# A fused mixer layer on one core: GpSimd's two-input steps of a head pair and the output weights' buffers in the Projection stage

## The chip, the cores and the metric

The kernel runs on one core of a Trainium2 chip. The metric is the device time of one execution in microseconds (us). Before the change three runs took 1478.3, 1480.67 and 1480.91 us; the median is 1480.67 us. The engines are TensorE (PE; its weight loads are shown apart as PEld), VectorE (DVE), ScalarE (ACT), GpSimd (POOL) and SyncE (SP), which issues the transfers.

## The reference

One layer over 2048 tokens with 1024 features, all in float32. The input is normalised and multiplied by `w_in` (1024 x 3712); the columns of that product feed three mixers; their outputs, each gated, go through `w_out`, and a gated addition of a second input follows.

```python
h = rms_norm(x, pre_norm_g[i])
z = h @ w_in[i]
out_a = spatial_gating(u_a, v_a, ...) * silu(g_a)
out_b = conv_module(val_b, glu_b, ...) * silu(g_b)        # 31 taps
out_c = rwkv7_mix(z[..., oc:og], ...) * silu(z[..., og:]) # 8 heads of 64
mix = concatenate([out_a, out_b, out_c], -1) @ w_out[i]
x = x + rms_norm(mix, post_norm_g[i])
gate = sigmoid(x @ ple_gate_w[i] + ple_gate_b[i])
x = x + (p[i] @ ple_w[i]) * gate
```

In `rwkv7_mix` the columns r, k, v are first mixed with the token before (`z + mu * (prev - z)`); then `kk = k * k_k` is divided by its norm per head, `k` is scaled by `1 + (a - 1) * k_a`, and the scan over time takes `-kk`, `kk * a`, `k`, `v` and `r`.

## The kernel before

The program has three stages. **Projection** computes `z` and all that is made of it for the mixers. A second stage runs the scan in chunks of 64 tokens, and the last one multiplies by `w_out` and applies the gate. The change is in Projection only.

Projection works on two halves of 1024 tokens. `z` is made transposed, 128 columns by 1024 tokens, in 29 column tiles in the order of the list `ORDER` (2, 8, 3, 6, 24, 9, 7, 12, 16, 13, 20, 17, 21, 4, 14, ...). Tiles 2 and 3 are made by L312 (`gemm_t`) in another layout; every other one by L300 (`gemm1`) in 48 matmuls of 128 x 512. Each operand is held as the sum of a high and a low part of a shorter type, so a tile takes three products, and every operand must first be split: ScalarE copies the high part and a two-input subtraction makes the low one. For the weights this is done in half 0 (`load_w`, L282 on ScalarE and L283 on GpSimd); both parts go to DRAM (`w_s`), and half 1 reads them back (`again`, L292), two buffers of the pool `w` for each tile. The pool `w` has 6 buffers of 512 KB, so three tiles' weights fit. `z` has two PSUM buffers: the gemm of a tile can start only when every reader of the tile two places earlier is done.

What reads a tile differs. `s_prep` (one for each of the four head pairs and each half) takes the tiles of r, k and v: `shift` (L329 on ScalarE, L330 and L333 on VectorE) is the token shift, and about twenty elementwise steps follow, five of them on GpSimd in the kernel before: the low part of the squares `rn` (`parts`, L232), `rn * ic` (L522), `ks * ic` (L524), `ks * em` (L527) and the low part of `rs` (L232 again). `sums` (L240) multiplies such parts by a matrix of ones on TensorE. `s_lora` shifts tile 24 into a buffer of the pool `mk` and splits it (L424 to L431). `s_conv` multiplies a tile by its gate (L444) and adds 31 taps on VectorE (L449 and 30 times L453) for each of two tiles. `s_sgu` normalises tiles 2 and 3 (L583 to L587).

`s_wout` splits the output weights: eight parts of 128 x 1024, each loaded (L378), copied by ScalarE (L380), subtracted on GpSimd (L381) and both parts written to DRAM (L383). It does so at the start of half 1 in three buffers of the pool `mk` each; this pool has 8 buffers.

In Projection a scheduler sets the order in which each engine gets its instructions. Every one of these generators yields a due time in units of one tile (half 1 begins at `NG`, 29), and lowers it for what must be done early by `at(...)`: the readers of a `z` tile are put at its time minus 5. An engine runs its queue strictly in the order so made, and a buffer is given to its next user in that order too. From the second stage on the order of PE and DVE is written out.

Of the kernel before, what the change touches and what calls it, by code (L numbers as in the profile page):

```python
# [12 lines left out]
F32R = mybir.dt.float32r  # L13
AF = mybir.ActivationFunctionType
ALU = mybir.AluOpType
# [19 lines left out]
def hybrid_kernel(ctx, tc, x, x_t, w_in, vecs, wup, pw_w, sgu_wt, sgu_lnb, sgu_b,  # L35
                  w_out, post_g, p_t, ple_w, gate_w, gate_b, out):
    nc = tc.nc
# [17 lines left out]
    def nm(s):  # L55
        uid[0] += 1
        return f"{s}{uid[0]}"

    def new(tag, shape=(128, 1024), dt=F32):
        return sb.tile(list(shape), dt, tag=tag, bufs=BUFS[tag], name=nm(tag))  # L60
# [81 lines left out]
    def col(i):  # L142
        return vc[:, i:i + 1]
# [84 lines left out]
    def parts(src, eng):  # L228

        hl = [new("mk", dt=F32R) for _ in range(2)]  # L230
        nc.scalar.copy(hl[0], src)
        eng.tensor_tensor(out=hl[1], in0=src, in1=hl[0], op=ALU.subtract)  # L232
        return hl
# [93 lines left out]
    def shift(j, half, z, tag="L"):  # L327
        o = new(tag)
        nc.scalar.activation(o, z, AF.Identity, scale=om[:, j:j + 1])  # L329
        nc.vector.scalar_tensor_tensor(out=o[:, 1:], in0=z[:, :HT - 1], scalar=col(V_MU + j), in1=o[:, 1:],  # L330
                                       op0=ALU.mult, op1=ALU.add)
        if half == 1:
            nc.vector.scalar_tensor_tensor(out=o[:, 0:1], in0=zl[:, j:j + 1], scalar=col(V_MU + j),  # L333
                                           in1=o[:, 0:1], op0=ALU.mult, op1=ALU.add)
        else:
            nc.scalar.copy(zl[:, j:j + 1], z[:, HT - 1:HT])
        return o
# [4 lines left out]
    def split(dst_hi, dst_lo, src):  # L342

        nc.scalar.copy(dst_hi, src)
        nc.vector.tensor_tensor(out=dst_lo, in0=src, in1=dst_hi, op=ALU.subtract)
# [4 lines left out]
    NG = len(ORDER)  # L350
# [22 lines left out]

    def s_wout():
        for k in range(8):
            yield NG + 1.2 + 0.4 * k
            wr = new("mk")
            nc.sync.dma_start(out=wr, in_=w_out[k * 128:(k + 1) * 128, :])  # L378
            ws = [new("mk", dt=F32R) for _ in range(2)]
            nc.scalar.copy(ws[0], wr)  # L380
            nc.gpsimd.tensor_tensor(out=ws[1], in0=wr, in1=ws[0], op=ALU.subtract)  # L381
            for j in range(2):
                nc.sync.dma_start(out=wo_s[k, :, j], in_=ws[j].bitcast(F32))  # L383

# [71 lines left out]
    def s_prep(half, p, st):  # L456
# [6 lines left out]
        ic = new("mk")  # L463
# [20 lines left out]
        em = new("L")  # L484
# [5 lines left out]
        rs_ = shift(p, half, Z[half, 12 + p])  # L490
        yield b0 + TG[16 + p] + 0.1
        at(b0 + TG[16 + p] - 5)
        ks_ = shift(4 + p, half, Z[half, 16 + p])
        yield b0 + TG[16 + p] + 0.0

        rn = new("mk")
        nc.scalar.activation(rn, ks_, AF.Square, scale=col(V_KK + p))
        hl = parts(rn, nc.gpsimd)
        for g in range(2):
            sp = mps()  # L500
            sums(sp, ones64, [hl], slice(g * 512, (g + 1) * 512))
# [11 lines left out]
        for g in range(2):  # L513
# [3 lines left out]
                                           in1=ep[:, c8, 0:64], op0=ALU.mult, op1=ALU.mult)  # L517
# [1 line left out]
            c0 = 16 * half + 8 * g  # L519
            nc.sync.dma_start(out=ar_s[c0:c0 + 8, :, p, :].rearrange("c p s -> p c s"), in_=ar)  # L520

        nc.gpsimd.tensor_tensor(out=rn, in0=rn, in1=ic, op=ALU.mult)  # L522
        nc.scalar.activation(ic, ic, AF.Identity, scale=col(V_KA + p), bias=om[:, 13 + p:14 + p])
        nc.gpsimd.tensor_tensor(out=ks_, in0=ks_, in1=ic, op=ALU.mult)  # L524
        yield b0 + TG[20 + p] + 1.3
        nc.vector.tensor_tensor(out=rn, in0=rn, in1=em, op=ALU.mult)
        nc.gpsimd.tensor_tensor(out=em, in0=ks_, in1=em, op=ALU.mult)  # L527
        for par in range(2):
            lo = 64 * par
            dst = bk_s[16 * half:16 * half + 16, lo:lo + 64, p, :, :].rearrange("c p k s -> p k c s")  # L530
# [10 lines left out]
        for par in range(2):  # L541
            nc.sync.dma_start(
                out=v_s[t0:t0 + HT, par, p, :].rearrange("(i t) d -> t i d", t=128),
# [2 lines left out]

        nc.vector.scalar_tensor_tensor(out=rs_, in0=rs_, scalar=col(V_RK + p), in1=ks_,
                                       op0=ALU.mult, op1=ALU.mult)
        hl = parts(rs_, nc.gpsimd)
        for g in range(2):  # L550
            sp = mps()
            sl = slice(g * 512, (g + 1) * 512)
# [115 lines left out]

    S = []
    S += [s_weights(), s_wout(), s_x(), s_gemm(), s_silu(0), s_const()]  # L670
    for half in range(2):
        st = {}
        S += [s_lora(half, st), s_conv(half, 0, st), s_conv(half, 1, st)]
        S += [s_prep(half, p, st) for p in range(4)]
        S += [s_sgu(half, st), s_pw(half, st)]
# [677 lines left out]
```

## Time and profile before

| what | us |
|---|---|
| median of three runs | 1480.67 |
| the profiled execution's own time | 1478.66 |
| its span (first to last instruction) | 1476.9 |
| TensorE busy | 1386.2 |
| VectorE busy | 1000.6 |
| ScalarE busy | 573.7 |
| GpSimd busy | 374.0 |

The mean granted clock of TensorE was 0.977 of full speed. All times in the rows are counted from the start of the span. Half 0 of Projection runs to about 430 us (its last gemms still run beside the first work of half 1), half 1 to about 740 us. A timeline groups neighbouring instructions of one line: a row gives the start, the sum of their durations (with the gaps between them), the engine, line and operation, and in brackets the idle time of the engine before it and who released it. `z<-h,w` means a result in a buffer named z from buffers h and w.

### The profile page before, as it was taken

What the parts mean: (1) busy time and instruction counts of PE and PEld (TensorE: products, weight loads), DVE (VectorE), ACT (ScalarE), POOL (GpSimd) and SP (SyncE); (2) the same over time, 40 slices, a digit from 0 to 9 for tenths busy, and PEclk for the clock granted to TensorE, in tenths of its full rate; (3) what the DMA queues carried; (4) which work ended last, traced back from release to release, by engine and by line L of the source; (5) the groups of instructions that cost most, each with busy time, mean ns of one, the idle gap of its engine ahead of it and who ended that gap; (6) DMA issues with size and microseconds to landing.
All of it is one profiled execution on the core that took longest, in us unless ns stands there. A gap on an engine that the chain in (4) does not pass through costs nothing.

```text
span 1476.9 us, 24431 instructions
## 1 busy us (share of the span) xinstructions
PE 1386.2 (94%) x9701; PEld 1105.7 (75%) x9701; DVE 1000.6 (68%) x1955; ACT 573.7 (39%) x900; POOL 374.0 (25%) x332
## 2 busy tenths in 40 slices
PE   7998989999998499999899989999999989999998
PEld 6876767787796377778667777777777777888887
DVE  6599993674437999535975687787788653555553
ACT  6333344555331352634333435444543443212121
POOL 5432454541403303403320112202211100111110
PEclk9999999999999699999999989999999999999999
DMA  8332366679538415635842653323332443323231
GB/s 325 144 142 86 128 197 202 185 255 312 187 124 306 150 64 161 170 109 171 256 144 80 231 192 98 116 82 116 95 101 73 139 141 123 134 102 130 101 132 43
DMA packets 158312, 223.30 MB, mean 151 GB/s; under 512 B 58236, under 2 KB 108149, under 8 KB 158198
## 3 DMA queue, kind: packets, MB, share of 16 engines
q1 hardware_dynamic: 158066, 221.68, 45.3%
q8 instruction: 76, 1.25, 0.4%
q14 instruction: 38, 0.31, 0.1%
q10 hardware_dynamic: 132, 0.06, 0.0%
HBM read 132.58 MB, written 89.13 MB: 150 GB/s over the span
## 4 chain that ended last, share of the span: by engine, by line
PE 66%; DVE 26%; ACT 3%; issue 2%; DMA 2%; POOL 1%; DVEq 0%; ACTq 0%; POOLq 0%
PE z L300 26%; PE z L1165 12%; DVE inv L453 10%; PE z L1052 8%; PE c L1142 3%; PE z L312 3%; DVE inv L874 3%; PE m L821 2%; DVE inv L879 2%; DVE mk L245 2%; PE m L240 1%; DVE inv L862 1%; PE m L1121 1%; PE c L944 1%; PE c L932 1%
## 5 line engine op out<-in xcount | busy, mean ns | idle before, releaser
L300 PE MATMUL z<-h,w 128*128 128x512 f32 x2592 | 638.2, 401 | 31.4 <-DVE mk L330 23.2
L300 PEld LDWEIGHTS z<-h,w 128*128 128x128 f32 x2592 | 487.9, 190 | 152.2 <-DVE mk L330 23.6
L1052 PE MATMUL z<-h,w 128*128 128x512 f32 x768 | 206.4, 412 | 0.7 <-DVE w L1039 0.7
L453 DVE SCALAR_TENSOR_TENSOR inv<-inv,vc,inv 128x1024 f32<-128x1024 f32 x120 | 195.2, 1635 | 2.6
L1052 PEld LDWEIGHTS z<-h,w 128*128 128x128 f32 x768 | 140.1, 192 | 31.7 <-DVE w L1039 1.1
L283 POOL TENSOR_TENSOR w<-w,w 128x1024 fp32r<-128x1024 f32 x26 | 70.4, 2709 | 126.8 <-PE z L300 93.8
L1165 PE MATMUL z<-L,w 128*128 128x512 f32 (+1 forms) x384 | 96.1, 393 | 0.0
L1165 PE MATMUL z<-h,w 128*128 128x512 f32 (+1 forms) x384 | 93.6, 392 | 0.8 <-DVE inv L1148 0.8
L1109 POOL TENSOR_TENSOR inv<-inv,pg 128x1024 f32<-128x1024 f32 x16 | 38.5, 2405 | 216.3 <-DMA inv<-mx_s 141.3
L1149 ACT ACTIVATE inv<-inv 128x512 f32<-128x512 f32 (+1 forms) x33 | 20.4, 619 | 182.5 <-DVE inv L1148 182.5
L874 DVE TENSOR_TENSOR inv<-inv,inv 128x48 f32<-128x48 f32 (+23 forms) x464 | 85.8, 219 | 2.3
L879 DVE TENSOR_TENSOR inv<-inv,inv 128x48 f32<-128x48 f32 (+23 forms) x464 | 84.2, 217 | 1.2
L1165 PEld LDWEIGHTS z<-h,w 128*128 128x128 f32 x384 | 71.5, 189 | 17.3 <-DVE inv L1148 1.2
L1148 DVE TENSOR_TENSOR inv<-z,L 128x512 f32<-128x512 f32 (+1 forms) x32 | 21.9, 683 | 89.1 <-PE z L1165 89.1
L1165 PEld LDWEIGHTS z<-L,w 128*128 128x128 f32 x384 | 70.3, 188 | 15.2
L979 POOL TENSOR_TENSOR ri<-ri,pc 128x256 f32<-128x256 f32 x31 | 19.5, 628 | 239.6 <-DVE L L977 229.4
L245 DVE RECIPROCAL mk<-mk 128x256 f32<-128x256 f32 x40 | 65.9, 1709 | 17.5 <-ACT mk L504 9.5
L826 DVE TENSOR_TENSOR mk<-m,mask 128x512 f32<-128x512 f32 x58 | 37.6, 685 | 35.4 <-PE m L821 31.2
L830 ACT COPY inv<-mk 32x128 f32<-32x128 f32 x128 | 37.8, 295 | 52.1 <-DVE mk L826 49.3
L330 DVE SCALAR_TENSOR_TENSOR L<-z,vc,L 128x1023 f32<-128x1023 f32 x24 | 30.6, 1277 | 38.8 <-ACT L L329 36.6
L312 PE MATMUL z<-w,h 128*128 128x256 f32 x384 | 53.4, 295 | 0.9 <-ACT h L262 0.9
L329 ACT ACTIVATE L<-z,om 128x1024 f32<-128x1024 f32 x24 | 26.8, 1115 | 69.3 <-PE z L300 69.3
(246 smaller groups left out, 2067.5 us busy)
## 6 DMA issues: line engine op xcount, KB each, us to landing
w_s<-w SPq DMA_DIRECT2D x58, 512.0 KB, 3.4
w<-w_s SPq DMA_DIRECT2D x58, 512.0 KB, 5.0
w<-in_w_in_dram SPq DMA_DIRECT2D x26, 512.0 KB, 3.6
L<-in_x_dram SPq DMA_DIRECT2D x16, 512.0 KB, 8.1
ar_s<-L SPq DMA_DIRECT2D x16, 512.0 KB, 5.8
wo_s<-mk SPq DMA_DIRECT2D x16, 512.0 KB, 4.8
L<-ar_s SPq DMA_DIRECT2D x32, 256.0 KB, 3.1
L<-bk_s SPq DMA_DIRECT2D x32, 256.0 KB, 4.1
```

What stands on the lines that cost most here:

```text
L245: nc.vector.reciprocal(t[:, g * 256:(g + 1) * 256], t[:, g * 256:(g + 1) * 256])
L283: nc.gpsimd.tensor_tensor(out=ws[1], in0=wr, in1=ws[0], op=ALU.subtract)
L300: nc.tensor.matmul(z[:, g * 512:(g + 1) * 512], lhsT=ws[a][:, k * 128:(k + 1) * 128], rhs=h[:, b, k, :], start=(n == 0), stop=(n == 23))
L312: nc.tensor.matmul(z[:, i * 256:(i + 1) * 256], lhsT=h[:, b, k, i * 128:(i + 1) * 128], rhs=ws[k // 4][a][:, (k % 4) * 256:(k % 4 + 1) * 2 ...
L453: nc.vector.scalar_tensor_tensor(out=ac, in0=y[:, i:i + HT], scalar=col(V_CW + 2 * i + ct), in1=ac, op0=ALU.mult, op1=ALU.add)
L830: nc.scalar.copy(g["g"][32 * q:32 * q + 32, 0, 4 * ci:4 * ci + 4, :], mk[32 * q:32 * q + 32, par, :, s0:s0 + 32])
L874: nc.vector.tensor_tensor(out=tmp[:, o:o + n, :m], in0=tl[:, lo:hi, m:m + 1].to_broadcast([128, n, m]), in1=ml[:, m, :m].unsqueeze(1).to_b ...
L879: nc.vector.tensor_tensor(out=tl[:, lo:hi, :m], in0=tl[:, lo:hi, :m], in1=tmp[:, o:o + n, :m], op=ALU.add)
L1052: nc.tensor.matmul(mx[:, nh * 512:(nh + 1) * 512], lhsT=oT[a][:, k, :], rhs=wo[k // 4][:, b, k % 4, nh * 512:(nh + 1) * 512], start=(k == ...
L1109: nc.gpsimd.tensor_tensor(out=x2, in0=x2, in1=pg[0], op=ALU.mult)
L1142: nc.tensor.matmul(pp, lhsT=pT[:, a, k, :], rhs=gw[8 + k][b][:, nh * 512:(nh + 1) * 512], start=(n == 0), stop=(n == 5))
L1165: nc.tensor.matmul(z, lhsT=xT[a][:, k, :], rhs=gw[k][b][:, sl], start=(k == 0 and n == 0), stop=(k == 7 and n == 2))
```

## The change

Five steps per head pair, 40 in all, that GpSimd computed (L232 for `rn` and for `rs_`, L522, L524, L527) are VectorE's. The eight parts of the output weights get due times of NG + 2.3 + 1.5k in place of NG + 1.2 + 0.4k, take their three buffers from the pool `w` in place of `mk`, and their low part is made by `split`, which is ScalarE and VectorE. On GpSimd `load_w`'s subtractions (L283), `s_lora`'s (L431) and some small work stay in Projection. From line 376 on, a line of the changed kernel has a number lower by one (L381 goes, and L452 is the taps' line that was L453); `split`'s lines are L344 and L345.

```diff
     def s_wout():
         for k in range(8):
-            yield NG + 1.2 + 0.4 * k
-            wr = new("mk")
+            yield NG + 2.3 + 1.5 * k
+            wr = new("w")
             nc.sync.dma_start(out=wr, in_=w_out[k * 128:(k + 1) * 128, :])
-            ws = [new("mk", dt=F32R) for _ in range(2)]
-            nc.scalar.copy(ws[0], wr)
-            nc.gpsimd.tensor_tensor(out=ws[1], in0=wr, in1=ws[0], op=ALU.subtract)
+            ws = [new("w", dt=F32R) for _ in range(2)]
+            split(ws[0], ws[1], wr)
             for j in range(2):
                 nc.sync.dma_start(out=wo_s[k, :, j], in_=ws[j].bitcast(F32))
...
-        hl = parts(rn, nc.gpsimd)
+        hl = parts(rn, nc.vector)
...
-        nc.gpsimd.tensor_tensor(out=rn, in0=rn, in1=ic, op=ALU.mult)
+        nc.vector.tensor_tensor(out=rn, in0=rn, in1=ic, op=ALU.mult)
         nc.scalar.activation(ic, ic, AF.Identity, scale=col(V_KA + p), bias=om[:, 13 + p:14 + p])
-        nc.gpsimd.tensor_tensor(out=ks_, in0=ks_, in1=ic, op=ALU.mult)
+        nc.vector.tensor_tensor(out=ks_, in0=ks_, in1=ic, op=ALU.mult)
         yield b0 + TG[20 + p] + 1.3
         nc.vector.tensor_tensor(out=rn, in0=rn, in1=em, op=ALU.mult)
-        nc.gpsimd.tensor_tensor(out=em, in0=ks_, in1=em, op=ALU.mult)
+        nc.vector.tensor_tensor(out=em, in0=ks_, in1=em, op=ALU.mult)
...
-        hl = parts(rs_, nc.gpsimd)
+        hl = parts(rs_, nc.vector)
```

The order on ScalarE at the start of half 1. A number behind a name tells buffers of one pool apart; mk_3334 and mk_3286 are the shifted tile 24 in the kernel before and after, mk_3037 the first conv tile's gate, rs the reciprocal deviation of `s_sgu`. Before:

```order
L380 CAST mk_3041<-mk_3039 128x1024
L380 CAST mk_3053<-mk_3051 128x1024
L185 ACT_TABLE_LOAD
L185 ACTIVATE rs_3164<-mv_135,epsr 128x4
L380 CAST mk_3061<-mk_3059 128x1024
L380 CAST mk_3185<-mk_3183 128x1024
L380 CAST mk_3197<-mk_3195 128x1024
L380 CAST mk_3259<-mk_3257 128x1024
L380 CAST mk_3271<-mk_3269 128x1024
L380 CAST mk_3279<-mk_3277 128x1024
L329 ACTIVATE mk_3334<-z_3285,om 128x1024
L424 ACT_TABLE_LOAD
```

After:

```order
L438 ACTIVATE mk_3037<-z_2988 128x1024
L185 ACT_TABLE_LOAD
L185 ACTIVATE rs_3140<-mv_135,epsr 128x4
L344 CAST w_3161<-w_3159 128x1024
L329 ACTIVATE mk_3286<-z_3237,om 128x1024
L344 CAST w_3231<-w_3229 128x1024
L423 ACT_TABLE_LOAD
```

Before, all eight copies of output weights stand ahead of the shift of tile 24 (L329). After, one of them does; the others stand later.

The order on VectorE behind the normalisation of tile 3 (L587 before, L586 after), where inv_3255 and inv_3223 are the sum of the first conv tile's taps. Before:

```order
L444 TENSOR_TENSOR inv_3252<-z_3203,mk_3037 128x1024
L587 TENSOR_SCALAR mk_134<-z_3067,mv_135,rs_3164 128x256 x4
L449 TENSOR_SCALAR inv_3255<-inv_3252,vc 128x1024
L443 COPY inv_3458<-halo 128x30
L453 SCALAR_TENSOR_TENSOR inv_3255<-inv_3252,vc,inv_3255 128x1024 x23
L330 SCALAR_TENSOR_TENSOR mk_3334<-z_3285,vc,mk_3334 128x1023
L333 SCALAR_TENSOR_TENSOR mk_3334<-zl,vc,mk_3334 128x1
L453 SCALAR_TENSOR_TENSOR inv_3255<-inv_3252,vc,inv_3255 128x1024 x7
```

After:

```order
L586 TENSOR_SCALAR mk_134<-z_3043,mv_135,rs_3140 128x256 x4
L345 TENSOR_TENSOR w_3162<-w_3159,w_3161 128x1024
L443 TENSOR_TENSOR inv_3220<-z_3171,mk_3037 128x1024
L448 TENSOR_SCALAR inv_3223<-inv_3220,vc 128x1024
L442 COPY inv_3418<-halo 128x30
L452 SCALAR_TENSOR_TENSOR inv_3223<-inv_3220,vc,inv_3223 128x1024 x7
L330 SCALAR_TENSOR_TENSOR mk_3286<-z_3237,vc,mk_3286 128x1023
L333 SCALAR_TENSOR_TENSOR mk_3286<-zl,vc,mk_3286 128x1
L452 SCALAR_TENSOR_TENSOR inv_3223<-inv_3220,vc,inv_3223 128x1024 x5
L345 TENSOR_TENSOR w_3232<-w_3229,w_3231 128x1024
L452 SCALAR_TENSOR_TENSOR inv_3223<-inv_3220,vc,inv_3223 128x1024 x7
```

Before, 23 taps stand ahead of tile 24's L330; after, seven do, and one subtraction of output weights (L345).

The order of transfers on SyncE at the same place, L292 being the two parts of a tile's weights for half 1. Before:

```order
L378 DMA mk_3039<-in_w_out_dram 128x1024
L383 DMA wo_s<-mk_3041 128x1024
L378 DMA mk_3051<-in_w_out_dram 128x1024
L292 DMA w_3047<-w_s 128x1024
L292 DMA w_3048<-w_s 128x1024
L383 DMA wo_s<-mk_3042 128x1024
L292 DMA w_3191<-w_s 128x1024
L292 DMA w_3192<-w_s 128x1024
L383 DMA wo_s<-mk_3053 128x1024
L378 DMA mk_3059<-in_w_out_dram 128x1024
L383 DMA wo_s<-mk_3054 128x1024
```

After:

```order
L378 DMA w_3159<-in_w_out_dram 128x1024
L382 DMA wo_s<-w_3161 128x1024
L292 DMA w_3167<-w_s 128x1024
L382 DMA wo_s<-w_3162 128x1024
L292 DMA w_3168<-w_s 128x1024
L292 DMA w_3225<-w_s 128x1024
L292 DMA w_3226<-w_s 128x1024
L378 DMA w_3229<-in_w_out_dram 128x1024
L382 DMA wo_s<-w_3231 128x1024
L292 DMA w_3298<-w_s 128x1024
L382 DMA wo_s<-w_3232 128x1024
```

After, a part's transfers stand between the two parts of a tile's weights (w_3167 and w_3168, w_3298 and w_3299), and the write of its low part, which waits for VectorE's L345, stands ahead of the second of them.

## Rows read from the trace of the kernel before

**Rows 1.** The page's first part: busy time, share of the span and instructions of each engine.

```profile
PE 1386.2 (94%) x9701; PEld 1105.7 (75%) x9701; DVE 1000.6 (68%) x1955; ACT 573.7 (39%) x900; POOL 374.0 (25%) x332
```

**Rows 2.** The timeline of TensorE at the start of half 1.

```profile
440.56 11.36 PE L300 MATMUL z<-h,w 128*128 128x512 f32 x48
453.24 22.57 PE L300 MATMUL z<-h,w 128*128 128x512 f32 x96 [1.32 <-DVE inv L444]
499.01 14.08 PE L300 MATMUL z<-h,w 128*128 128x512 f32 x48 [23.20 <-DVE mk L330]
```

**Rows 3.** Windows of that place: from and to, length, then the busy time (and instructions) of PE, PEld, DVE, ACT and POOL, the granted clock of TensorE, the share of the DMA engines and GB/s.

```profile
440.56:452.00 11.44, 11.36 (x50) 8.82 (x48) 1.92 (x10) 2.63 (x3) 2.40 (x1) 1.00 0.98 342
475.80:499.00 23.20, 0.01 (x1) 0.00 (x0) 22.77 (x15) 4.15 (x4) 8.80 (x3) 0.61 0.63 230
499.00:513.10 14.10, 14.09 (x49) 11.31 (x50) 13.01 (x8) 6.74 (x6) 5.00 (x3) 0.79 0.00 0
513.10:527.00 13.90, 13.90 (x57) 10.13 (x57) 13.35 (x11) 6.29 (x8) 0.00 (x0) 1.00 0.22 75
```

**Rows 4.** The timeline of VectorE there.

```profile
451.96 1.23 DVE L444 TENSOR_TENSOR inv<-z,mk 128x1024 f32<-128x1024 f32 x1 [6.62 <-PE z L300]
...
457.52 40.25 DVE L453 SCALAR_TENSOR_TENSOR inv<-inv,vc,inv 128x1024 f32<-128x1024 f32 x23
497.68 1.28 DVE L330 SCALAR_TENSOR_TENSOR mk<-z,vc,mk 128x1023 f32<-128x1023 f32 x1
```

**Rows 5.** The timeline of ScalarE there, and below it the group of the eight copies (busy time, mean ns of one, idle time before them by releaser).

```profile
453.36 1.05 ACT L380 CAST mk<-mk 128x1024 fp32r<-128x1024 f32 x1 [8.22 <-DMA mk<-in_w_out_dram]
...
489.79 1.04 ACT L380 CAST mk<-mk 128x1024 fp32r<-128x1024 f32 x1 [6.32 <-DMA mk<-in_w_out_dram]
490.74 1.11 ACT L329 ACTIVATE mk<-z,om 128x1024 f32<-128x1024 f32 x1
...
L380 ACT CAST mk<-mk 128x1024 fp32r<-128x1024 f32 x8 | 8.4, 1048 | 50.6 <-DMA mk<-in_w_out_dram 50.6
```

**Rows 6.** Two pieces of the chain that ended last (start, length, what): two taps one after the other.

```profile
461.48 1.30 DVE inv L453
...
462.80 3.31 DVE inv L453
```

**Rows 7.** The timeline of GpSimd at the same moment.

```profile
461.90 3.11 POOL L381 TENSOR_TENSOR mk<-mk,mk 128x1024 fp32r<-128x1024 f32 x1 [4.97 <-ACT mk L380]
```

**Rows 8.** Groups of instructions by line: the steps of GpSimd that the change moves, and two of VectorE of the same kind and size.

```profile
L527 POOL TENSOR_TENSOR L<-L,L 128x1024 f32<-128x1024 f32 x8 | 26.6, 3331 | 4.1 <-DVE mk L526 3.7
...
L232 POOL TENSOR_TENSOR mk<-mk,mk 128x1024 fp32r<-128x1024 f32 x8 | 22.5, 2808 | 83.1 <-ACT mk L231 83.1
L381 POOL TENSOR_TENSOR mk<-mk,mk 128x1024 fp32r<-128x1024 f32 x8 | 22.2, 2777 | 76.2 <-ACT mk L380 76.2
L522 POOL TENSOR_TENSOR mk<-mk,mk 128x1024 f32<-128x1024 f32 x8 | 22.1, 2769 | 78.4 <-DVE L L516 78.4
L524 POOL TENSOR_TENSOR L<-L,mk 128x1024 f32<-128x1024 f32 x8 | 21.9, 2738 | 8.1 <-ACT mk L523 8.1
...
L232 POOL TENSOR_TENSOR mk<-L,mk 128x1024 fp32r<-128x1024 f32 x8 | 19.2, 2400 | 45.1 <-ACT mk L231 34.6 <-PE z L300 10.5
...
L611 DVE TENSOR_TENSOR mk<-mk,mk 128x1024 f32<-128x1024 f32 x4 | 4.9, 1225 | 0.1
L345 DVE TENSOR_TENSOR h<-w,h 128x1024 fp32r<-128x1024 f32 x4 | 4.8, 1223 | 10.2 <-ACT h L344 10.2
```

**Rows 9.** Windows of four longer stretches, columns as in rows 3.

```profile
66.00:216.00 150.00, 140.10 (x570) 108.77 (x568) 146.32 (x102) 57.03 (x65) 55.04 (x22) 0.95 0.39 135
452.00:500.00 48.00, 23.56 (x98) 18.83 (x99) 47.21 (x33) 8.13 (x8) 17.42 (x6) 0.80 0.74 261
500.00:590.00 90.00, 89.68 (x368) 69.90 (x367) 85.00 (x67) 35.55 (x37) 21.75 (x8) 0.97 0.32 99
600.00:740.00 140.00, 135.77 (x619) 106.85 (x619) 84.04 (x74) 64.00 (x66) 40.28 (x22) 0.98 0.65 186
```

**Rows 10.** The timeline of TensorE in half 0: three of its waits.

```profile
186.12 0.72 PE L300 MATMUL z<-h,w 128*128 128x512 f32 x2 [3.20 <-ACT zl L336]
...
188.24 1.22 PE L240 MATMUL m<-mk,ones 128*128 128x512 f32 x2 [1.41 <-ACT mk L231]
...
201.96 1.25 PE L538 MATMUL m<-ident,L 128*128 128x128 f32 x8 [1.17 <-DVE mk L502]
```

**Rows 11.** The timeline of TensorE at the end of Projection.

```profile
731.71 0.98 PE L240 MATMUL m<-mk,ones 128*128 128x512 f32 x2 [1.18 <-ACT mk L231]
...
734.14 1.22 PE L240 MATMUL m<-mk,ones 128*128 128x512 f32 x2 [1.45 <-POOL mk L232]
...
736.96 3.63 PE L604 MATMUL m<-yc,mk 128*64 128x128 f32 x32 [1.60 <-DVE L L554]
```

**Rows 12.** The page's list of DMA issues (KB each, median us from issue to landing) for half 1's weights and the output weights; below it the same list for 430 to 450 us alone.

```profile
w<-w_s SPq DMA_DIRECT2D x58, 512.0 KB, 5.0
...
mk<-in_w_out_dram SPq DMA_DIRECT2D x8, 512.0 KB, 5.8
...
w<-w_s SPq DMA_DIRECT2D x4, 512.0 KB, 9.5
```

**Rows 13.** The waits of SyncE's queue from 420 to 700 us: who waited for whom, us in total, times, the longest.

```profile
SPq L292 <- PE z L300: 134.2, 15, 18.7
```

## Prediction

> **What bounds the kernel now.** I read first the busy times of the whole span: TensorE is busy 1386.2 of 1476.9 us, VectorE 1000.6, GpSimd 374.0 [rows 1]. So time can be won only where TensorE stands idle or runs at its lower clock, and moving 40 steps from one lightly loaded engine to another matters only if one of TensorE's waits changes. Then I read TensorE's timeline for those waits. One stands out: at the start of half 1 it is idle for 23.20 us, released by VectorE's L330, and a tile before it for 1.32 us [rows 2]. The windows show what follows: the granted clock is 1.00 before the wait, 0.61 in it and 0.79 in the first tile behind it, which takes 14.08 us where the tile at full clock took 11.36 [rows 2, 3]. (Those shares mean that part of the tile ran at 1.2 and the rest at 2.4 GHz.)
>
> Next I read who holds L330 up. VectorE works through 23 conv taps, 40.25 us, and only then comes to L330, at 497.68 [rows 4]. In that window it is busy 22.77 of 23.20 us [rows 3], so it isn't waiting: the order of its queue is the cause. The same L330 needs ScalarE's L329, and this stood behind the copies of the output weights: the last of them began at 489.79, after 6.32 us of waiting for its transfer, and the eight together waited 50.6 us [rows 5]. So two queues, each by itself, hold tile 24's `z` until about 490 or later, and the gemm of tile 7 needs that buffer when tile 9 ends, at 453.24 + 22.57 = 475.8 [rows 2].
>
> **The wait in half 1.** By the order of the changed kernel both causes go. On ScalarE one copy stands ahead of L329, not eight; on VectorE seven taps stand ahead of L330, not 23. Tile 24's `z` also took the buffer that L444 frees, since L444 (451.96) stood ahead of tile 3's normalisation; now that normalisation comes first, needs nothing later than tile 3, and frees its buffer before tile 6 ends. So the 1.32 us go too. When is L330 done in the new order? Tile 24 then starts at 452.0 and ends at 452.0 + 11.36 = 463.4. VectorE starts the conv at 452.0 with 1.23 us for the gating [rows 4]; the first tap and seven more, at 1.30 each [rows 6], take 10.4, so it is free at about 463.7. L329 takes 1.11 [rows 5] from 463.4, L330 1.28 [rows 4] behind it, to 465.8. The gemm of tile 7 wants the buffer at 463.4 + 11.36 = 474.7. That is 9 us of slack, nearly seven taps, so I take the whole wait as gone: 23.2 + 1.3, and with no idle TensorE the clock has no reason to fall, 14.08 − 11.36 = 2.7. Together 27.2 us. If the clock fell all the same, 2.7 would stay; that is the lower bound of this term's last part.
>
> What is late next there? The other stretch in which the DMA share is high lies just before: 0.98 at 342 GB/s from 440.56 to 452.00 [rows 3], because all eight parts were asked for at once. That is spread out now.
>
> **What the moved steps cost VectorE.** GpSimd took 2.40 to 3.33 us for each; VectorE's own subtractions and products of that size take 1.22 [rows 8]. 48 steps (40, and the 8 low parts of the output weights) are 48 x 1.22 = 59 us more on an engine that has 476 us free in the span, but hardly any in two places: it is busy 146.32 of 150 us in half 0 from 66 to 216, and 47.21 of 48 and 85.00 of 90 in half 1 from 452 to 590 [rows 9]. Against the cost stands what GpSimd took from VectorE. A tap takes 1.30 us alone and 3.31 beside GpSimd's 3.11 us subtraction [rows 6, 7], that is 2.0 us more. So a step that ran beside such a VectorE instruction gives back 2.0 for 1.22, and one that ran beside anything else gives back nothing: between −0.8 and +1.2 us of VectorE time each.
>
> From 452 to 500 GpSimd ran six low parts [rows 9]; with five or six of them beside taps that is about 10 to 12 us of VectorE's time, against three of 1.22 that the new order puts there. From 500 to 590 GpSimd ran eight instructions [rows 9], so at most eight moved steps, and about five of the output weights' subtractions are new: (8 + 5) x 1.22 = 15.9 us at most, against 5.0 of idle time, up to 2.0 given back for each step that met a tap, and the 23 us that the taps no longer cost TensorE. I cost this at nothing, because the taps themselves are what can wait: they are due long before anything reads their sum, and the order puts each tile's L330 between them. If that cover is gone, the price is the rival below.
>
> In half 0 three waits of TensorE for a chain through VectorE or ScalarE, 3.20, 1.41 and 1.17, lie where VectorE is full [rows 9, 10]; that is 5.8 us. The steps of the first head pair lie there, each giving back between 0.8 and taking 1.2. Between no gain and 5.8 I take a third, 2.0, since the weights' splits stay on GpSimd and go on stretching taps there, so only part of the lateness can go.
>
> At the end of Projection three waits of 1.18, 1.45 and 1.60 stand behind the last head pair [rows 11]. There the steps are a chain (`rn`, `ks`, `em`, `rs` and its low part), VectorE isn't full, and each is shorter by 2.40 − 1.22 = 1.2 us at least, but what TensorE waits for last is partly ScalarE's. Of 4.2 us I take 0.2; the ends are 0 and 4.2.
>
> **What the output weights' buffers cost.** Half 1's weights come through the pool `w`, two of six buffers for a tile, and SyncE waits there for the end of a gemm, 134.2 us in 15 times: so the transfers were held back by buffers, three tiles deep [rows 13]. Each part now takes three of the six for a while. The order shows the worst of it: the second half of a tile's weights is asked for behind a write that waits for VectorE's subtraction. For tile 9: the subtraction can start when tile 6 ends, at 452.0, ends at 453.2, the transfer behind it takes 5.0 [rows 12] and is there at 458.3; the gemm needs it at 463.4. The margin is 5 us. With the longer landing of 9.5 us of the crowded time [rows 12] it is there at 462.8, still in time by half a microsecond. I cost it at nothing, between 0 and what the slower rival gives.
>
> **The sum.** 23.2 + 1.3 + 2.7 + 2.0 + 0.2 = 29.4 us off the profiled execution's own 1478.66 (1476.9 of span and 1.8 around it) gives 1449.3. That execution lies 2.0 below the median of the three runs, so against that I predict 1451.
>
> **Rivals.**
>
> *VectorE becomes late later in half 1.* If no stretch is given back, VectorE has 15.9 − 5.0 = 10.9 us too much by 590, and tiles' L330 hand that on to TensorE: 1451 + 11 = 1462. For it: VectorE is full there [rows 9]. Against it: the order leaves the taps between the L330s, and stretches do go. The Trainium skill ("Perfetto Trace Analysis", Optimizing Scalar/DVE Operations) speaks for this rival: where VectorE is saturated it would move work off it, and it warns that moves between VectorE and GpSimd may not help as they share a read port. The rows at hand show the shared part in the tap of 3.31 us, and say that at these durations the move toward VectorE is about even.
>
> *The wait stays.* If something not in the order kept L330 from running before 490, the 27.2 us would stay and only small terms move: 1478 to 1482, no change. Against it stand the orders of both queues, which name the 23 taps and eight copies; nothing speaks for it but that a scheduler's order may meet a buffer I didn't follow.
>
> *Slower: weights wait for VectorE.* A part's subtraction stands in VectorE's queue behind taps, SyncE's queue waits for it, and behind that stand the next tile's weights. Were VectorE late at each of the eight parts by seven taps, 7 x 1.30 = 9.1 us, the margin of 5.0 would be overdrawn by 4.1 each time: 8 x 4.1 = 33 us, 3.4 more than the whole gain of 29.4, so 1484. It decides from 5.0 + 29.4/8 = 8.7 us of lateness at each part. For it: one part of the weights does hang on VectorE now, and landing takes 9.5 us in crowded time. Against it: the subtractions stand early among the taps, and the parts are 1.5 tiles apart, so that a late one can recover.
>
> **How the numbers follow.** My forecast, all of half 1's wait gone and no new one above a few us (1443 to 1457), has 0.70. VectorE or some weights late by 6 to 20 us (1457 to 1474) has 0.17; still faster. The wait stays: 0.04. Slower by weights: 0.06. Better than 1443: 0.03. The low end, 1443, is the forecast with half 0's other 3.8 and the end's other 4.0 gone too: 1451 − 7.8. The high end, 1464, is the first rival's 1462 and some 2 us for the clock behind a new wait. What a measurement can tell from no change is 0.2%, 3 us here. So faster 0.90, same 0.04, slower 0.06.
>
> **What would show it.** Right: TensorE's timeline from 440 to 530 has no wait above 2 us, tile 7's gemm takes about 11.4 us at clock 1.00, VectorE's L330 for tile 24 comes at about 465, taps beside which GpSimd rested take 1.3. Wrong: TensorE's waits in half 1 name L292's transfers (weights) or L330 again (VectorE), or stretched taps are as many as before; in half 0, waits near 186 to 202 us above 5.8 in sum would say that VectorE lost more than it got back.

## The result and the profile after

The changed kernel took 1441.19 us (median of four runs, 1437.73 to 1442.79), the kernel before 1479.49 beside it: a ratio of 0.974, 95% interval 0.9715 to 0.9766, so 38.3 us less. Forecast were 29.4 us less, to 1451, with a range down to 1443. The sign and the main term were right; the gain came out 9 us larger, and the time lies 2 us below the range.

The profiled execution after took 1437.73 us (span 1436.0), 40.9 us less than the profiled one before. Where they came from is read by setting the starts of the same gemm (the matmuls of one tile) side by side in the two traces: tile 6 of half 1 starts at 440.56 before and at 428.58 after, 12.0 us earlier; the second tile behind the old wait at 513.92 and 474.18, 39.7 us earlier; `s_sgu`'s first matmul in half 1, which has the last wait of [rows 11] (L604 before, L603 after), at 736.96 and 697.93, 39.0 us earlier; the last 1.9 us come later. So half 1's start gave 27.8 us, half 0 gave 12.0, and the end of Projection took 0.7 back.

The busy times of the changed kernel:

```profile
PE 1378.8 (96%) x9701; PEld 1102.1 (77%) x9701; DVE 1009.2 (70%) x2003; ACT 568.6 (40%) x897; POOL 246.0 (17%) x284
```

Against [rows 1] GpSimd lost 128 us and VectorE has only 8.6 more, though it runs 48 more instructions, nearly all of 1.2 us. TensorE was busy 7.4 us less with the same 9701 matmuls, since fewer of them ran at the lower clock (mean granted clock 0.987, before 0.977).

TensorE at the start of half 1, which answers to [rows 2]:

```profile
426.80 1.94 PE L312 MATMUL z<-w,h 128*128 128x256 f32 x15
428.58 44.77 PE L300 MATMUL z<-h,w 128*128 128x512 f32 x192
473.20 0.40 PE L469 MATMUL c<-pg,ri 128*128 128x512 f32 x1
```

The timeline joins 192 matmuls, four tiles, in one row without a bracket: both waits are gone, and 44.77 / 4 = 11.2 us is a tile's time at full clock. VectorE there, which answers to [rows 4]:

```profile
439.85 1.22 DVE L345 TENSOR_TENSOR w<-w,w 128x1024 fp32r<-128x1024 f32 x1 [6.88 <-issue]
440.99 1.22 DVE L443 TENSOR_TENSOR inv<-z,mk 128x1024 f32<-128x1024 f32 x1
442.25 0.82 DVE L448 TENSOR_SCALAR inv<-inv,vc 128x1024 f32<-128x1024 f32 x1
442.97 0.18 DVE L442 COPY inv<-halo 128x30 f32<-128x30 f32 x1
443.10 9.21 DVE L452 SCALAR_TENSOR_TENSOR inv<-inv,vc,inv 128x1024 f32<-128x1024 f32 x7
452.23 1.28 DVE L330 SCALAR_TENSOR_TENSOR mk<-z,vc,mk 128x1023 f32<-128x1023 f32 x1
```

Seven taps in 9.21 us, each 1.3, and L330 behind them at 452.23, 1.35 us after tile 24 ended (450.88). Tile 7 wanted the buffer at 462.04: 8.5 us of slack. ScalarE, which answers to [rows 5]:

```profile
433.44 1.05 ACT L344 CAST w<-w 128x1024 fp32r<-128x1024 f32 x1 [2.62 <-DMA w<-in_w_out_dram]
451.08 1.12 ACT L329 ACTIVATE mk<-z,om 128x1024 f32<-128x1024 f32 x1 [16.59 <-PE z L300]
454.57 1.05 ACT L344 CAST w<-w 128x1024 fp32r<-128x1024 f32 x1 [2.37 <-DMA w<-in_w_out_dram]
```

L329 now waits for the gemm and not for a copy. Windows of half 1 and of the full stretch of half 0, which answer to [rows 3, 9]:

```profile
428.58:439.73 11.15, 11.15 (x51) 9.05 (x49) 3.78 (x13) 1.35 (x2) 0.00 (x0) 1.00 0.37 150
439.73:485.00 45.27, 45.27 (x192) 35.60 (x191) 42.60 (x35) 13.91 (x14) 6.59 (x3) 1.00 0.59 197
485.00:575.00 90.00, 90.00 (x388) 71.27 (x387) 85.94 (x81) 37.78 (x39) 0.26 (x2) 1.00 0.62 190
66.00:216.00 150.00, 145.51 (x608) 113.28 (x607) 147.76 (x112) 61.93 (x72) 41.96 (x16) 0.98 0.46 154
```

VectorE is as full as before (42.60 of 45.27, 85.94 of 90, 147.76 of 150), yet TensorE has no wait in half 1 before 690 us: here a full engine was no bound, because what it had to hand over on time (tile 24's L330 above) stood early in its queue. In half 0 VectorE is busy for the same share, but 112 instructions fit where 102 did, and TensorE's clock is 0.98 where it was 0.95.

The waits left in half 0 and at the end of Projection, which answer to [rows 10, 11]:

```profile
141.34 1.22 PE L240 MATMUL m<-mk,ones 128*128 128x512 f32 x2 [3.38 <-ACT mk L231]
186.18 0.73 PE L240 MATMUL m<-mk,ones 128*128 128x512 f32 x2 [0.83 <-DVE mk L232]
...
691.43 0.98 PE L240 MATMUL m<-mk,ones 128*128 128x512 f32 x2 [1.18 <-ACT mk L231]
695.07 1.22 PE L240 MATMUL m<-mk,ones 128*128 128x512 f32 x2 [2.65 <-DVE mk L232]
697.93 2.40 PE L603 MATMUL m<-yc,mk 128*64 128x128 f32 x20 [1.64 <-DVE L L553]
```

SyncE's queue from 420 to 660 us, which answers to [rows 13], and the transfers of [rows 12]:

```profile
SPq L292 <- PE z L300: 51.4, 12, 13.6
...
w<-w_s SPq DMA_DIRECT2D x58, 512.0 KB, 5.4
...
w<-in_w_out_dram SPq DMA_DIRECT2D x8, 512.0 KB, 7.2
```

No gemm waits for weights, though each part takes three of the six buffers of the pool `w` for a while.

### The profile page after: what moved, and what is told of

Same layout as the page of the kernel before. It is cut to its first block, busy times and chain, and to the rows that moved or that the text cites. A ratio compares the mean times of both kernels' runs of the same rounds, so it can differ in the third digit from the quotient of the medians.

```text
span 1436.0 us, 24389 instructions
## 1 busy us (share of the span) xinstructions
PE 1378.8 (96%) x9701; PEld 1102.1 (77%) x9701; DVE 1009.2 (70%) x2003; ACT 568.6 (40%) x897; POOL 246.0 (17%) x284
## 4 chain that ended last, share of the span: by engine, by line
PE 73%; DVE 20%; ACT 3%; issue 2%; DMA 1%; DVEq 0%; ACTq 0%
PE z L300 33%; PE z L1164 12%; PE z L1051 8%; DVE inv L452 5%; PE c L1141 3%; PE z L312 3%; DVE inv L873 3%; PE m L820 3%; DVE inv L878 2%; PE m L240 1%; DVE mk L245 1%; DVE inv L861 1%; PE m L1120 1%; DVE L L976 1%; DMA w<-in_gate_w_dram 1%
## 5 line engine op out<-in xcount | busy, mean ns | idle before, releaser
L452 DVE SCALAR_TENSOR_TENSOR inv<-inv,vc,inv 128x1024 f32<-128x1024 f32 x120 | 173.0, 1460 | 1.4
L283 POOL TENSOR_TENSOR w<-w,w 128x1024 fp32r<-128x1024 f32 x26 | 74.3, 2857 | 235.9 <-PE z L300 178.1
L1108 POOL TENSOR_TENSOR inv<-inv,pg 128x1024 f32<-128x1024 f32 x16 | 38.3, 2394 | 216.9 <-DMA inv<-mx_s 117.6
L245 DVE RECIPROCAL mk<-mk 128x256 f32<-128x256 f32 x40 | 65.8, 1708 | 12.1 <-ACT mk L637 8.0
L820 PE MATMUL m<-L,L 64*128 64x128 f32 x464 | 44.5, 299 | 10.1 <-DVE yn L1002 8.6
L312 PEld LDWEIGHTS z<-w,h 128*128 128x128 f32 x384 | 50.3, 197 | 3.1 <-ACT h L262 1.6
```

What stands on the lines that cost most here:

```text
L245: nc.vector.reciprocal(t[:, g * 256:(g + 1) * 256], t[:, g * 256:(g + 1) * 256])
L312: nc.tensor.matmul(z[:, i * 256:(i + 1) * 256], lhsT=h[:, b, k, i * 128:(i + 1) * 128], rhs=ws[k // 4][a][:, (k % 4) * 256:(k % 4 + 1) * 2 ...
L452: nc.vector.scalar_tensor_tensor(out=ac, in0=y[:, i:i + HT], scalar=col(V_CW + 2 * i + ct), in1=ac, op0=ALU.mult, op1=ALU.add)
L820: nc.tensor.matmul(sp[par][:, p, :], lhsT=bk[lo:lo + 64, p, :], rhs=ar[lo:lo + 64, p, :], start=True, stop=True)
L1108: nc.gpsimd.tensor_tensor(out=x2, in0=x2, in1=pg[0], op=ALU.mult)
```

## Experiments

Theory after the result: the order of two queues made half 1's wait, and the steps on GpSimd made VectorE's instructions beside them longer (below: stretch); in the full places of half 0 that was the lateness that TensorE saw, with a lower clock behind it. The rival on half 0: GpSimd's own latency, its 2.4 to 3.3 us for a step that others wait for.

**Each part alone.** The output weights' part alone is the changed kernel with the five steps back on GpSimd:

```diff
-        hl = parts(rn, nc.vector)
+        hl = parts(rn, nc.gpsimd)
...
```

> The output weights' part of the change alone (later due times, buffers from w, low part on VectorE); the forty steps stay on GpSimd. If the wait of 23.20 us in half 1 came from the place of the eight copies and the 23 taps in two queues, it goes here as in the changed kernel: 27 us less than before, about 1452, and half 0 keeps its waits (12.7 us in sum). Rival: the moved steps were needed in half 1 as well, because beside GpSimd's steps VectorE is late there; then TensorE waits again for L330 between 500 and 600 and the time is 1456 to 1468.

Measured: 1463.89, ratio 0.9881 (0.986 to 0.9903). The wait is gone and 27.3 us are won by the second tile behind it, as expected; but 11 of them are lost again between 560 and 627 us. TensorE there:

```profile
565.05 0.73 PE L240 MATMUL m<-mk,ones 128*128 128x512 f32 x2 [1.59 <-POOL mk L232]
573.50 1.26 PE L537 MATMUL m<-ident,L 128*128 128x128 f32 x8 [1.42 <-DVE mk L501]
594.89 0.50 PE L469 MATMUL c<-mk,ri 128*128 128x512 f32 x1 [1.14 <-ACT L L476]
605.78 0.73 PE L300 MATMUL z<-h,w 128*128 128x512 f32 x2 [1.39 <-DVE L L330]
609.62 1.22 PE L240 MATMUL m<-mk,ones 128*128 128x512 f32 x2 [2.89 <-ACT mk L231]
```

and VectorE there:

```profile
547.85 3.42 DVE L452 SCALAR_TENSOR_TENSOR inv<-inv,vc,inv 128x1024 f32<-128x1024 f32 x1
551.20 1.21 DVE L345 TENSOR_TENSOR w<-w,w 128x1024 fp32r<-128x1024 f32 x1
552.33 3.44 DVE L452 SCALAR_TENSOR_TENSOR inv<-inv,vc,inv 128x1024 f32<-128x1024 f32 x1
...
559.35 3.43 DVE L546 SCALAR_TENSOR_TENSOR L<-L,vc,L 128x1024 f32<-128x1024 f32 x1
```

Between 520 and 620 us six taps take over 2 us, in the changed kernel none. In the kernel before the same place had one such tap and no wait above 0.4 us: VectorE had done 23 taps before tile 7 began [rows 4], here twelve. So the rival is right here: the wait goes for its full price only with the steps moved.

The steps alone (the changed kernel with `s_wout` of the kernel before):

```diff
-            yield NG + 2.3 + 1.5 * k
-            wr = new("w")
+            yield NG + 1.2 + 0.4 * k
+            wr = new("mk")
...
-            split(ws[0], ws[1], wr)
+            nc.scalar.copy(ws[0], wr)
+            nc.gpsimd.tensor_tensor(out=ws[1], in0=wr, in1=ws[0], op=ALU.subtract)
```

> The forty steps on VectorE alone; the output weights as before. If half 0's gain (12 us between the starts of the same gemms in the two traces) belongs to the steps, this takes 1479.5 - 12 = about 1467, with the wait of 23 us at the start of half 1 still there. Rival: half 0's gain belongs to something else, such as a clock that fell in the one profiled execution; then 1476 to 1480.

Measured: 1463.86, ratio 0.9885 (0.9865 to 0.9904), 17.5 less by the medians and 14.7 between the traced executions. By the start of tile 6 in half 1 its trace is 12.1 us ahead, half 0's gain, and the wait of 23.64 us stands as before. About 2 us more come in half 1. Of the 12 us, 1.6 lie before 57 us, where nothing is changed: in the profiled execution of the kernel before the clock was 0.92 from 35 to 57 us, and the second trace of the changed kernel (below) is as late there. That is chance, so half 0's gain by the change is 12.0 − 1.6 = 10.4 us. The other traces bear it out, counted in the same way from 57 us: the eight others that have these steps on VectorE in half 0, and no further edit there, reach that gemm 8.3 to 10.4 us ahead of the kernel before, and the three with the steps on GpSimd 0.9 to 2.1 behind it.

The later due times alone, in the kernel before:

```diff
-            yield NG + 1.2 + 0.4 * k
+            yield NG + 2.3 + 1.5 * k
```

> The kernel before with the later due times alone: buffers from mk and GpSimd's subtraction as before. If the order of the two queues was the whole cause of the 23.20 us, the due times alone take them away: about 1452. Rival: the buffers matter, since eight parts in mk hold back the other users of that pool; then part of the wait stays or comes later, 1458 to 1475.

Measured: 1469.29, 0.9918 (0.9896 to 0.9939). The due times alone take the whole wait away (28.5 us ahead behind it), but 16 us come back, the longest of the new waits 6.74 us at 582.86 for VectorE's L502. The changed kernel with the early due times (the same edit the other way):

> The changed kernel with the early due times (NG + 1.2 + 0.4k). Four copies stand ahead of the shift of tile 24, and each part takes three of the six w buffers while half 1's weights need the same ones. If the weights were the margin (5 us of it in the changed kernel), TensorE now waits for weights at the first tiles of half 1: 8 parts within 3 tiles take 24 buffers where 6 tiles' weights need 12, so at least one gemm's length of wait for every two parts, 1455 to 1485. Rival: buffers come round fast enough and only the order matters: 1441 to 1450.

Measured: 1462.88, 0.989 (0.9849 to 0.9931). The waits for weights came, four of them. ScalarE, SyncE and TensorE there, and below them two of SyncE's waits from 440 to 480 us:

```profile
453.54 1.04 ACT L344 CAST w<-w 128x1024 fp32r<-128x1024 f32 x1 [5.28 <-DMA w<-in_w_out_dram]
...
455.02 1.21 SPq L292 DMA_DIRECT2D w<-w_s  x2
...
460.93 13.87 PE L300 MATMUL z<-h,w 128*128 128x512 f32 x48 [9.88 <-DVE inv L452]
481.25 13.27 PE L300 MATMUL z<-h,w 128*128 128x512 f32 x46 [2.12 <-DMA w<-w_s]
496.35 0.74 PE L300 MATMUL z<-h,w 128*128 128x512 f32 x2 [1.17 <-DMA w<-w_s]
498.85 1.56 PE L300 MATMUL z<-h,w 128*128 128x512 f32 x5 [1.76 <-DMA w<-w_s]
...
SPq L382 <- ACT w L344: 25.3, 5, 7.7
SPq L382 <- DVE w L345: 6.4, 4, 3.6
```

The profile puts the 9.88 us down to a tap (L452), which ended last, at 460.88; but no gemm reads a tap. TensorE's queue also waited for the first of its weights, which SyncE asked for at 455.02 and which landed at 460.80. SyncE came to it only behind the write of a part's high part (L382), which waited for ScalarE's copy at 453.54, and this for the part's own load. So the slower rival's price, weights late behind the parts, is real, and the later due times are what keeps it away; but SyncE waited here for ScalarE's copies (25.3 us) more than for VectorE's subtractions (6.4), which the rival named.

The parts late, low part on VectorE, but in `mk`:

```diff
-            wr = new("w")
+            wr = new("mk")
-            ws = [new("w", dt=F32R) for _ in range(2)]
+            ws = [new("mk", dt=F32R) for _ in range(2)]
```

> The changed kernel with the output weights' parts through the pool mk as before, but late and with the low part on VectorE. If due times and engines are all that counts, 1440 to 1445. Rival: eight parts of three buffers hold back mk's other users (the run with late due times alone gave back 15 us between 537 and 600, the one with the w buffers 11), so 1445 to 1450.

Measured: 1453.35, 0.9824 (0.9801 to 0.9848), above even the rival's range. ScalarE shows a reason: a copy of output weights waits 7.42 us for its transfer, and the sigmoids of a head pair stand behind it (TensorE then waits 4.71 us for L476).

```profile
575.05 1.04 ACT L344 CAST mk<-mk 128x1024 fp32r<-128x1024 f32 x1 [7.42 <-DMA mk<-in_w_out_dram]
576.11 1.28 ACT L476 ACT_TABLE_LOAD   x1
577.41 0.69 ACT L476 ACTIVATE L<-c,vc 128x512 f32<-128x512 f32 x1
```

It is the mechanism of [rows 5] again. So the pool `w` is worth 12 us of its own by the medians; by the starts of the same gemms 9 of them are lost in half 1.

**Half by half.** All five steps in this manner, and with `half == 1` in the second kernel:

```diff
-        hl = parts(rn, nc.vector)
+        hl = parts(rn, nc.vector if half == 0 else nc.gpsimd)
...
```

> The changed kernel with the steps on VectorE in half 0 only; in half 1 GpSimd has them. Half 0 as in the changed kernel; half 1 as with the output weights' part alone, where 11 us of waits came back between 560 and 620: about 1441 + 11 = 1452. Rival: that give-back came from half 0's lateness carried over; then 1441 to 1444.

Measured: 1453.54, 0.9821 (0.9789 to 0.9853), with five waits between 553 and 598 us like those of the first experiment.

> The changed kernel with the steps on VectorE in half 1 only; in half 0 GpSimd has them. Half 0's waits as before, half 1 clean: about 1441 + 10 = 1451. Rival as for the run with half 0 only: 1458 or more.

Measured: 1455.29, 0.9837 (0.9802 to 0.9872), with half 0's waits at 128, 142, 185, 187 and 201 us as in the kernel before and no wait in half 1 before the end of Projection. So each half's share stands by itself: some 12 us in half 1 and, in the trace, 11.4 in half 0.

**Stretch or latency.** Extra steps that nobody reads put work beside VectorE's on GpSimd again, but outside the chain that others wait for:

```diff
+    def ghost(t):
+        nc.gpsimd.tensor_tensor(out=gscr, in0=t[:, :896], in1=t[:, :896], op=ALU.add)
...
         hl = parts(rn, nc.vector)
+        ghost(hl[0])
...
         nc.vector.tensor_tensor(out=ks_, in0=ks_, in1=ic, op=ALU.mult)
+        for _ in range(3):
+            ghost(ks_)
...
         hl = parts(rs_, nc.vector)
+        ghost(hl[0])
```

> The changed kernel with forty more GpSimd steps that nobody reads: 128 x 896, two SBUF inputs, one behind each of the two low parts and three behind the products of a head pair, into a scratch buffer. The order on TensorE and VectorE is that of the changed kernel. If GpSimd's steps cost time by stretching VectorE's instructions beside them, VectorE is late again in its full places: half 0's gain of about 10 us goes and in half 1 up to 11 more, so 1449 to 1462, with taps above 3 us as in the kernel before. Rival: the cost was GpSimd's own latency in the chain and the queue of its steps; then nothing waits for the extra steps and the time stays 1440 to 1444.

Measured: 1449.15 (1448.3 to 1457.17), 0.9801 (0.9765 to 0.9838): 8 us more than the changed kernel, at the lower edge of what was expected. Its profiled execution is the slowest of the four; there, with the order of the changed kernel on TensorE and VectorE, half 0 has these waits:

```profile
193.07 1.22 PE L245 MATMUL m<-mk,ones 128*128 128x512 f32 x2 [6.51 <-DVE mk L237]
...
233.95 0.50 PE L474 MATMUL c<-mk,ri 128*128 128x512 f32 x1 [2.28 <-ACT mk L483]
...
237.27 1.22 PE L245 MATMUL m<-mk,ones 128*128 128x512 f32 x2 [2.39 <-ACT mk L236]
```

In the changed kernel the same places have 0.83, none and 0.97. L237 is `parts`' subtraction on VectorE, and from 181 us on VectorE reads:

```profile
181.81 2.70 DVE L534 TENSOR_TENSOR L<-L,L 128x1024 f32<-128x1024 f32 x1
184.42 2.70 DVE L554 SCALAR_TENSOR_TENSOR L<-L,vc,L 128x1024 f32<-128x1024 f32 x1
187.04 2.69 DVE L457 SCALAR_TENSOR_TENSOR inv<-inv,vc,inv 128x1024 f32<-128x1024 f32 x1
189.66 3.36 DVE L237 TENSOR_TENSOR mk<-mk,mk 128x1024 fp32r<-128x1024 f32 x1
```

Four instructions of 1.2 to 1.3 us take 11.4 in a row, three beside extra steps whose result nobody reads, the last beside a weight's subtraction (L288, 188.62 to 191.93) that they pushed back. So stretch alone can cost half 0 its time, 15.4 us in this trace; the other three executions took 1448 to 1450 in all, some 8 us more than the changed kernel. Latency isn't needed for it; whether it had a share in the kernel before wasn't tested. In half 1 the same extra steps cost this trace only 1.3 us by the starts of the same gemms. That left half 1's 12 us open, and three more kernels went at it. Twice as many extra steps in half 1 alone (the edit above with two `ghost` calls for each, under `half == 1`):

> The changed kernel with two extra GpSimd steps (128 x 896, read by nobody) for each of the twenty of half 1, none in half 0; VectorE's order is that of the changed kernel. If half 1's 12 us (the price of leaving the steps on GpSimd there) come from stretched instructions of VectorE alone, twice as many steps beside VectorE bring back 6 to 12 us: 1447 to 1453. Rival: they come from GpSimd's own 2.4 to 3.4 us in the chain that TensorE waits for; then 1440 to 1444.

Measured: 1447.73, 0.9796 (0.9765 to 0.9827); by the starts of the same gemms 5 us are lost in half 1. Then, with the edit by halves, the two low parts alone and the three products alone on GpSimd in half 1:

> The changed kernel with the two low parts of a head pair in half 1 on GpSimd (eight steps), the three products on VectorE. TensorE's sums wait for these low parts directly. If the chain's latency is half 1's price, most of the 12 us come back: 1449 to 1453. If stretch is, two fifths at most: 1441 to 1446.

Measured: 1443.42 (1440.12 to 1447.24), 0.9762 (0.9728 to 0.9795).

> The changed kernel with the three products of a head pair in half 1 on GpSimd (twelve steps), the low parts on VectorE. The products lead only to transfers and to the step before rs. If stretch is half 1's price, about three fifths of the 12 us come back: 1447 to 1450. If the chain to TensorE's sums is, little does: 1441 to 1444.

Measured: 1446.53 (1439.82 to 1447.35), 0.9772 (0.9739 to 0.9805). By the medians the low parts, which TensorE's sums wait for, cost some 2 us and the products 5. But the traces lose most of their time where nothing is changed: from the start of the last tile's gemm, which runs beside the second stage, to the end they take 658.0 and 655.9 us, the changed kernel 649.1 and in its second trace (below) 653.4. By the starts of the same gemms to the end of half 1 the low parts cost nothing and the products 1.5. So latency as the main price falls. Stretch by itself brings back 1.3 of the 12 us with as many extra steps, and 5 with twice as many. The parts alone don't add up to the 12 of all five; that lateness has first to use up VectorE's slack would fit, but isn't shown, and the cause of half 1's 12 us stays open.

**GpSimd's other steps.** The 26 low parts of half 0's weights also stretch VectorE's instructions:

```diff
-            nc.gpsimd.tensor_tensor(out=ws[1], in0=wr, in1=ws[0], op=ALU.subtract)
+            nc.vector.tensor_tensor(out=ws[1], in0=wr, in1=ws[0], op=ALU.subtract)
```

> The changed kernel with the 26 low parts of half 0's weights on VectorE too, so that GpSimd has hardly a step left in Projection. By the price that the traces give (1.2 us on VectorE for each, and 2.0 back for each that ran beside a VectorE instruction with two SBUF inputs) VectorE has about as much to do as now: 1438 to 1444. Rival: VectorE is full in half 0 from 66 to 200 us and each step is 1.2 more, eleven in that place, 13 us: 1448 to 1454.

Measured: 1448.14, 0.978 (0.9754 to 0.9807): a time in the rival's range, but not for its reason. By the starts of the same gemms it loses 4.1 us before 60 us, where VectorE makes `h` (TensorE waits 0.63, 0.72 and 1.06 us for it), gains 7.0 by 147 us, in the place that was thought too full for eleven more steps, and loses 10 from 340 to 392 us, where a weight's low part stands late in VectorE's queue (5.50 us of waiting for L283 and the lower clock behind it). So a version with only the middle ones moved, beside the changed kernel again on the same chip:

```diff
-                    W[0, ct] = load_w(ct, tag="inv" if n == 2 else "w")
+                    W[0, ct] = load_w(ct, tag="inv" if n == 2 else "w", eng=nc.vector if 5 <= n <= 15 else None)
```

> The changed kernel once more, on the chip of the three kernels beside it: a ratio of 0.974, about 1441. Its trace has half 0's three waits of 3.4, 0.8 and 1.0 us.

Measured: 1441.57, 0.9746 (0.9722 to 0.9769). Its trace has 1.39 and 2.69 us at 129 and 143 us in place of one wait of 3.4, so that small waits fall differently from execution to execution.

> The changed kernel with the low parts of eleven tiles' weights (those split between about 60 and 200 us) on VectorE too; the others stay on GpSimd. The run with all 26 on VectorE won 7 us against the changed kernel up to 147 us and lost 4.8 before 60 us and 11 between 360 and 385 us. If the stretched taps are half 0's price (10 to 11 of 59 taps there above 2.0 us in the changed kernel), this keeps the gain without the losses: the wait of 3.4 us at 141 goes, 1435 to 1438. Rival: VectorE's eleven more steps at 1.2, 13 us, decide: 1445 or more.

Measured: 1434.04 (1432.51 to 1436.89), 0.9703 (0.968 to 0.9725), 7.5 less than the changed kernel on the same chip, and the fastest of all: its slowest execution is faster than the fastest of the changed kernel's eight. How much of the 7.5 is the edit's own is less sure. Of the 10.5 us between the two traces, 5.7 lie before half 1, 1.6 of them again before 57 us, and 4.8 behind the start of the last tile's gemm, where nothing is changed; so the traces show some 4. The taps tell what became of the stretch, in the kernel before, the changed kernel, the one with extra steps and this one:

```profile
L453 DVE SCALAR_TENSOR_TENSOR inv<-inv,vc,inv 128x1024 f32<-128x1024 f32 x120 | 195.2, 1635 | 2.6
```

```profile
L452 DVE SCALAR_TENSOR_TENSOR inv<-inv,vc,inv 128x1024 f32<-128x1024 f32 x120 | 173.0, 1460 | 1.4
```

```profile
L457 DVE SCALAR_TENSOR_TENSOR inv<-inv,vc,inv 128x1024 f32<-128x1024 f32 x120 | 179.4, 1512 | 1.4
```

```profile
L452 DVE SCALAR_TENSOR_TENSOR inv<-inv,vc,inv 128x1024 f32<-128x1024 f32 x120 | 156.4, 1322 | 1.3
```

With 1.30 us for a tap alone [rows 6], 1322 ns is nearly the unstretched mean: 39 us of the taps' time went with GpSimd's steps.

> As the run before it, and the last head pair's low part of rs back on GpSimd in half 1: in the changed kernel it stands behind four reciprocals (6.59 us) in VectorE's queue and TensorE waits 2.65 us for it, where the kernel before waited 1.45. So 1.2 us less than the run before it. Rival: TensorE waits as long for the step behind; no difference.

Measured: 1437.62 (1435.17 to 1440.33), 0.9722 (0.9699 to 0.9745), not faster. The wait for L232 is 1.51 us in place of 2.65, but two of 0.40 and 0.89 come behind it in place of one of 1.65, and its interval overlaps that of the run before it; a gain of 1.2 us can't be told here.

## Why the prediction was right in half 1 and too small in half 0

*The wait of half 1* (forecast 23.2 + 1.3 + 2.7 = 27.2) was right by its steps: 27.8 us in the trace, L330 began 1.35 us behind tile 24's end (forecast 464.5 − 463.4 = 1.1), 8.5 us of slack (forecast 9), tile time 11.2 at full clock. The cause was the order of the two queues: the due times alone take the wait away, and the moved steps alone leave 23.64 us of it. One reading beside it was wrong, without a term in the sum: the eight parts weren't asked for all at once, but one after the other from 429.85 to 483.87 us.

*VectorE from 452 to 590, costed at nothing*, held for the changed kernel: no wait of TensorE in half 1. But the reason given, that the taps can wait, was half of it. With the steps left on GpSimd the taps can't wait enough and 11 us are lost again. The moved steps aren't a side cost of this change there; they are what lets the other part keep its gain. The first rival was thus the fate of the output weights' part alone (1464), not of the whole change.

*Half 0, a third of 5.8, so 2.0,* is the step that failed. Measured: 10.4; even the low end of the range allowed it only 5.8. Three things were left out of that term. Its waits were too few and went almost whole: those of TensorE over 0.6 us in half 0 sum to 12.7 us before and 5.2 after (5.9 in the changed kernel's second trace). The three of [rows 10], 5.8, left 0.83, and 0.64 at 290, 1.02 at 370.6 and 1.15 at 395.7, the last one a wait for GpSimd's own L283, are gone. The clock wasn't priced there, though it was in half 1: from 186.1 to 206.1 the kernel before had 0.83, and the same matmuls take 15.1 us for 20.0 at a clock of 1.00, some 3 of it by the clock and the rest waits; with the 3.20 of the first wait, just ahead of it, that place alone gave 8.1. And the balance of VectorE was taken as about even with an open sign, where the trace could have told more.

That balance, by the whole span: 48 steps of about 1.21 us are 58 us more and VectorE is busy 8.6 us longer, so 49.5 us came back, 1.03 for a step. The bounds (−0.8 to +1.2 for each) hold with a mean of +0.18. In the full place of half 0 the mean is below nothing: the 102 instructions that the kernel before runs there [rows 9] take 9.2 us less in sum after the change, and six moved steps add 7.3. That the weights' splits "go on stretching taps" was right: of half 0's 60 taps 14 took over 2 us before and 11 after, and 2 once eleven splits went too. Yet TensorE's waits went almost whole with only three of these taps shortened, so that it was no reason for a third.

*The end of Projection, 0.2 less*, had the wrong sign: the three waits sum to 5.5 after and 4.2 before. The low part of the last `rs` stands behind four reciprocals (6.59 us) in VectorE's queue, where GpSimd had none ahead of it.

*The output weights' buffers at nothing*: right, no gemm waits for weights. The slower rival's price is seen when the parts come early (waits of 9.9, 2.1, 1.2 and 1.8 us for weights). What wasn't forecast is that `w` is needed: through `mk`, late parts hold ScalarE's queue and 9 to 12 us are lost again.

*The rule of the Trainium skill* ("Perfetto Trace Analysis", Optimizing Scalar/DVE Operations), by which work may be moved off a saturated VectorE, even to GpSimd, doesn't hold for this case: the move toward VectorE made it sooner done in its full place of half 0 (9.2 us back for 7.3 added). The warning beside it, that moves between those two might not help since they share a read port, agrees with the trace; here it speaks for the move, since a step on GpSimd that met a tap cost VectorE 2.0 us.

## What to carry to other kernels

Where VectorE is full, price a step on GpSimd at what it does to the VectorE instruction beside it: here 2.0 us of stretch where it met a tap, 1.0 on the mean of all 48, against 1.2 us for doing the step there. When a long wait of TensorE is removed, ask what other engines did in it: here VectorE had worked its taps off, and the wait's price was kept in full only because VectorE was relieved at the same time. Price the clock behind every wait, not behind the largest alone.

## What was not expected of the hardware

The stretch works both ways. In the changed kernel one of GpSimd's subtractions took 5.92 us, where most take 2.4. It began beside the last two taps of a row and VectorE's scan (L481, 2.32 us), which all kept their usual length, and only the tap behind the scan took 3.36:

```profile
114.76 5.92 POOL L283 TENSOR_TENSOR w<-w,w 128x1024 fp32r<-128x1024 f32 x1 [11.56 <-PE z L300]
```

And an engine with 147.76 of 150 us busy can do more work when it is given more: its busy share says how long instructions took, not how much was done.
